# A hybrid attention layer on one core: some rounded weights and constants come by casting DMAs, probabilities are normalised in place, pairs of heads share steps, and the written order is new

## The chip, the core and the metric

The kernel runs on one core of one Trainium2 chip. The core has TensorE (PE in the profile; its weight loads are the row PEld), VectorE (DVE), ScalarE (ACT), GpSimd (POOL) and SyncE (SP), a shared on-chip memory (SBUF) of 128 partitions, and the accumulators of TensorE (PSUM), here eight banks of 128x512 float32. DMAs are issued by SP, ACT or POOL and run on 16 DMA engines.

The metric is the device time of one execution in microseconds (us), the median of several runs. The kernel before took 612.99 us (three runs: 612.47, 612.99, 614.84).

## What is computed

One decoder layer for 512 tokens of width 1024, in float32:

```python
h = rms_norm(x, pre_mix_norm)
proj = h @ w_in                                   # 1024 x 3600
att_q, att_k, att_v, gdn_qkv, gdn_z, gdn_a, gdn_b = split(proj)
o_att = moba_attention(att_q, att_k, att_v, rel_bias)   # 8 heads of 64
o_gdn = gated_deltanet(gdn_qkv, gdn_z, gdn_a, gdn_b, conv_w, A_log, dt_bias, gdn_norm_w)
mix = concat([o_att, o_gdn]) @ w_out              # 1024 x 1024
x = x + rms_norm(mix, post_mix_norm)
h = rms_norm(x, pre_mlp_norm)
m = square(relu(h @ w_up)) @ w_down               # 1024 x 4096 x 1024
return x + rms_norm(m, post_mlp_norm)
```

With 512 tokens, blocks of 256 and three past blocks allowed, the attention is plain causal softmax attention with a relative-position bias. The gated DeltaNet cuts the tokens into eight chunks of 64, needs the inverse of a unit lower triangular 64x64 matrix for each chunk and head, and then carries a 64x64 state per head through the chunks (a scan).

## The kernel before

**Three products for one.** A float32 product is made of three matmuls on rounded parts (type fp32r): hi is the rounded operand, lo is the operand minus hi, and hi·hi + hi·lo + lo·hi is summed in PSUM (`mm3`, L144). So every weight block is loaded raw by a DMA of SP, rounded by ACT (hi), and subtracted by DVE or POOL (lo): `load_split` (L121), `begun`/`ended` (L128 to 139), `split` (L112).

**Stages.** `head` (L198) does the first four projections while the norm of x is summed; PE can begin when the first x block is rounded by ACT (L240) and the first weight block by DVE (L241). `projections` (L259) does 20 more column blocks (24 matmuls of 128x512 each) and, at the item w0, the attention values of all tokens (`by_token`, 96 matmuls). After each block an evacuation runs: `conv_silu` (L359) for the DeltaNet's q, k and v, which multiplies the PSUM block in place by the norm factor, then reads it on ACT and three more times on DVE, so that the bank (tag `ps_mm`, two banks) comes free only after the third; `take_z` (L428) and `take_a` (L620) for z and for the attention's q and k.

`turned` (L513) lays scalars of one pair of heads into R, turns R by four PE transposes and makes the rows RC; `chunks` (L551) uses them for a pair of heads and ends with the chunk matrices NT and AT. The last pair's mark lets `inverse` (L735) start: 31 steps of two DVE multiplications, with its data brought through DRAM on the way in and out. `scan` (L757) reads the result, does two rounds of small matmuls, and goes through the eight chunks; after each pair of chunks `finish_o` (L885) normalises 128 tokens (its norm factor is computed by four POOL operations, L891, L171, L175, L893).

`scores` (L647) goes over four pairs of heads and three groups of query blocks (3; 2; 1 and 0): matmuls, a DVE operation that adds the bias and takes the row minimum (L675), and the exponential on ACT with the row sums (L677). After all groups DVE takes the reciprocal of the sums (L681), ACT spreads them over 512 columns (L683). `values` (L688) turns the exponentials by PE transposes (L701), ACT copies them out (L704), the spread sums are turned by four more PE transposes (L720) and copied (L722), and after the product with V DVE multiplies by them (L728) and `split` makes hi and lo.

`weights_out` (L915) loads w_out in sixteen 128x512 blocks through `load_split` (raw buffers `wo_raw`, L926), `output` (L933) multiplies (half b=0 of the columns, then b=1, for token tiles 0 and 1, then 2 and 3), `normed` (L990) adds the residual and makes the normalised input of the MLP (its two norm factors by POOL's L171 and L175), `weights_up` (L1022) and `up0` (L1039) begin the MLP. The MLP (from L1110) follows a written order of its own on all engines.

**What sets the order.** The stages above are Python generators. A list of names (`STEPS`, L20) says which generator is advanced next (`Weave.run`, L58; a name whose wait is not yet met is passed over). PE executes exactly in the order in which this emits its instructions (`manual_schedule`, L79). DVE, ACT, POOL and SP are ordered by the framework's planner from estimated times and priorities; `LEAD` (L22) raises the priority of some generators. `ORDER` (L28) is the order of the column blocks, and `LO_DVE` (L29) says which half blocks n of the projections have their lo made by DVE instead of POOL (the others by POOL). Each engine executes its own list in order: an instruction that waits holds all behind it.

## Time and profile before

| | us |
|---|---|
| median of three runs | 612.99 |
| the profiled execution's own time | 613.28 |
| its span, first to last instruction | 611.5 |
| PE busy in the span | 600.7 |
| DVE / ACT / POOL busy | 481.2 / 364.8 / 140.9 |
| granted TensorE clock, mean | 0.999 of full |
| moved by DMAs | 113.21 MB, mean 185 GB/s |

Matmuls overlap in PE's pipeline, so the duration of one (about 390 ns for 128x512) is longer than its share of PE; the distance from one start to the next is what it costs (about 227 ns). A line of the program that is a helper's stands for all who call it: L82 is every matmul, L85 every transpose, so the tile names tell them apart. In timelines each row has start, duration, engine, line, operation, what is written and read, and in brackets the idle time before and what ended it.

### The profile page before, as it was taken

The page shows a single profiled execution, that of the slowest core. Times are in us where ns is not written, and L with a number is a line of the kernel's source. Part 1 is how long each engine was busy: PE and PEld are TensorE (multiplying, and loading weights), DVE is VectorE, ACT ScalarE, POOL GpSimd, SP SyncE. Part 2 cuts the span into 40 slices and gives each one's busy share as a digit, 9 for nine tenths or more (in the row PEclk, how much of TensorE's full clock was granted, in tenths as well). Part 3 has the DMA queues.
Part 4 walks back from the last instruction along what each step waited for, and adds up shares of the span by engine and source line. Part 5 has one row for each costly group of instructions (what it writes and reads, how often), then busy time and mean ns, then how long its engine had stood idle before and what let it go on. Part 6 is the DMA issues. An engine that isn't in the chain of part 4 may idle for free.

```text
span 611.5 us, 11058 instructions
## 1 busy us (share of the span) xinstructions
PE 600.7 (98%) x4281; PEld 515.0 (84%) x4281; DVE 481.2 (79%) x692; ACT 364.8 (60%) x645; POOL 140.9 (23%) x180
## 2 busy tenths in 40 slices
PE   9999999999999999999999999999999999999995
PEld 7778788877778786888999999999998888888884
DVE  6688975999664866668799888787798888887776
ACT  7379772353677567444368565755575657565663
POOL 1557745001221111025022231122221310000000
PEclk9999999999999999999999999999999999999999
DMA  9332334227412124815879899998999999767503
GB/s 316 89 115 86 88 87 117 91 70 184 125 45 66 35 89 128 286 53 173 329 176 311 219 274 223 273 283 205 235 337 357 285 293 286 254 229 297 164 0 138
DMA packets 61156, 113.21 MB, mean 185 GB/s; under 512 B 15784, under 2 KB 35368, under 8 KB 60720
## 3 DMA queue, kind: packets, MB, share of 16 engines
q1 hardware_dynamic: 43120, 82.89, 40.0%
q0 software_dynamic: 17696, 29.36, 23.2%
q8 instruction: 33, 0.54, 0.4%
q10 hardware_dynamic: 288, 0.26, 0.1%
q14 instruction: 19, 0.16, 0.1%
HBM read 106.71 MB, written 35.15 MB: 232 GB/s over the span
## 4 chain that ended last, share of the span: by engine, by line
PE 58%; issue 9%; DMA 2%; ACT 2%; DVE 0%; POOLq 0%; SPq 0%
PE ps_mm L82 27%; PE ps_g L82 17%; PE ps_a L82 13%; DMA xy<-d_x 1%; DMA wo_raw<-in_w_out 1%; PE ps_a L85 1%; ACT wo_h L125 0%; ACT ph L704 0%; ACT L L677 0%; DVE wo_l L126 0%; DVE wdl L114 0%; ACT wdh L113 0%; PE ps_g L85 0%; POOLq L1532 0%; ACT ot L876 0%
## 5 line engine op out<-in xcount | busy, mean ns | idle before, releaser
L113 ACT CAST wdh<-wd 128x1024 fp32r<-128x1024 f32 x53 | 55.9, 1054 | 51.4 <-PE ps_mm L82 22.6
L113 ACT CAST u_h<-w 128x1024 fp32r<-128x1024 f32 x49 | 50.9, 1044 | 52.1 <-DVE w L1146 15.6
L114 DVE TENSOR_TENSOR wdl<-wd,wdh 128x1024 fp32r<-128x1024 f32 x53 | 64.9, 1224 | 21.6 <-ACT wdh L113 21.4
L114 DVE TENSOR_TENSOR u_l<-w,u_h 128x1024 fp32r<-128x1024 f32 x49 | 59.8, 1224 | 23.8 <-ACT u_h L113 23.8
L82 PE MATMUL ps_mm<-hT_h,w_hi 128*128 128x512 f32 x168 | 71.3, 424 | 1.3 <-DVE conv L365 1.0
L82 PE MATMUL ps_mm<-hT_h,w_lo 128*128 128x512 f32 x168 | 66.1, 394 | 0.0
L1179 POOL DMA_DIRECT2D d_T<-in_w_down x32 | 33.0, 1032 | 142.3 <-DMA d_T<-in_w_down 81.3
L82 PE MATMUL ps_mm<-hT_l,w_hi 128*128 128x512 f32 x168 | 65.7, 391 | 0.0
L137 ACT CAST w_hi<-w_raw 128x512 fp32r<-128x512 f32 x50 | 31.0, 620 | 46.1 <-DMA w_raw<-in_w_in 12.0
L82 PE MATMUL ps_mm<-wdh,u_h 128*128 128x512 f32 x116 | 45.3, 390 | 0.0
L82 PE MATMUL ps_mm<-wdl,u_h 128*128 128x512 f32 x116 | 45.1, 389 | 0.0
L82 PE MATMUL ps_mm<-wdh,u_l 128*128 128x512 f32 x116 | 45.1, 389 | 0.0
L82 PEld LDWEIGHTS ps_mm<-hT_h,w_hi 128*128 128x128 f32 x168 | 31.7, 189 | 12.4 <-issue 5.9
L82 PEld LDWEIGHTS ps_mm<-hT_h,w_lo 128*128 128x128 f32 x168 | 31.5, 188 | 7.5 <-DVE w_lo L138 0.4
L82 PEld LDWEIGHTS ps_mm<-hT_l,w_hi 128*128 128x128 f32 x168 | 31.8, 189 | 4.9
L138 POOL TENSOR_TENSOR w_lo<-w_raw,w_hi 128x512 fp32r<-128x512 f32 x23 | 29.7, 1291 | 20.3 <-ACT w_hi L137 17.4
L114 DVE TENSOR_TENSOR u_l<-f,u_h 128x1024 fp32r<-128x1024 f32 x28 | 34.1, 1218 | 0.0
L82 PE MATMUL ps_g<-wdh,u_h 128*128 128x512 f32 x80 | 31.1, 389 | 0.0
L82 PE MATMUL ps_g<-wdl,u_h 128*128 128x512 f32 x80 | 31.1, 389 | 0.0
L82 PE MATMUL ps_g<-wdh,u_l 128*128 128x512 f32 x80 | 31.1, 389 | 0.0
L113 ACT CAST u_h<-f 128x1024 fp32r<-128x1024 f32 x28 | 29.3, 1046 | 0.0
L138 DVE TENSOR_TENSOR w_lo<-w_raw,w_hi 128x512 fp32r<-128x512 f32 x27 | 21.4, 794 | 7.9 <-ACT w_hi L137 7.8
(486 smaller groups left out, 1830.2 us busy)
## 6 DMA issues: line engine op xcount, KB each, us to landing
d_T<-in_w_down POOLq DMA_DIRECT2D x48, 512.0 KB, 11.0
wd<-d_T SPq DMA_DIRECT2D x32, 512.0 KB, 6.2
w<-in_w_up SPq DMA_DIRECT2D x28, 512.0 KB, 7.6
wd<-in_w_down SPq DMA_DIRECT2D x24, 512.0 KB, 7.3
w_raw<-in_w_in SPq DMA_DIRECT2D x40, 256.0 KB, 2.6
wo_raw<-in_w_out SPq DMA_DIRECT2D x16, 256.0 KB, 3.5
d_T<-d_T POOLq DMA_DIRECT2D x8, 512.0 KB, 12.1
ww<-in_w_first SPq DMA_DIRECT2D x8, 256.0 KB, 5.3
```

The lines of the kernel that those rows point to most:

```text
L82: nc.tensor.matmul(o, l, r, **kw)
L85: nc.tensor.transpose(o, i, ident[:k, :k])
L113: nc.scalar.copy(hi, src)
L114: tt(lo, src, f32(hi), op=OP.subtract)
L137: nc.scalar.copy(hi, raw)
L138: (sub or tt)(lo, raw, f32(hi), op=OP.subtract)
L1179: nc.gpsimd.dma_start(d_T[t][k], block(b, second)[k], accum_op=OP.add, max_dma_last_dim=1024)
```

## The change

- **First weights.** The rounded first block (`hi0`) comes by a DMA issued by POOL that casts float32 to fp32r; DVE's rounding is gone. The raw block is still loaded for lo.
- **Constants.** The selection matrix `sel` (now nine matrices instead of five) and the mask in RC come by three such DMAs instead of plain DMAs into temporaries, POOL copies and POOL memsets.
- **conv_silu** takes a source and a place for the scaled block: for v and for q3 the place is now SBUF, so PSUM is read once.
- **Joint visits.** `turned(z)` handles two pairs of heads in one set of transposes (R has 64 used rows); a new generator `matrices(z)` makes the chunk matrices of two pairs together. `take_v` waits for the joint mark.
- **Probabilities.** After each group the reciprocal of its sums is taken and POOL multiplies each row block of exponentials by it in place; the spread sums, their four transposes per pair, their copies and the multiplication after the product are gone.
- **w_out.** The rounded blocks come by eight casting DMAs of POOL, two blocks each (512 KB); the raw blocks are still loaded and lo still subtracted by DVE; the sixteen ACT roundings are gone, and the first half has four raw buffers instead of two.
- **normed.** The product with the norm weight is formed before the norm factor is known, the factor comes from ACT's square root and DVE's reciprocal, and the residual is added in the same DVE operation that applies it.
- **up0.** Three column tiles instead of four are computed for the first half of the tokens before the last tile is normalised; the fourth is computed for all 512 tokens at the end.
- `STEPS`, `LEAD`, `ORDER` and `LO_DVE` are new; LO_DVE (19, 68) gives four more lo blocks to DVE.

```diff
-ORDER = "k0 q0 x0 y0 k1 q2 q1 k2 k3 z0 q3 x1 w0 v3 v0 v1 v2 y1 y2 x2 x3 y3 z2 z3 z1"
-LO_DVE = (23, 51)
+ORDER = "k0 q0 x0 y0 k1 q2 q1 k3 k2 z0 x1 q3 w0 v3 v1 v0 y1 v2 x2 y2 y3 x3 z1 z3 z2"
+LO_DVE = (19, 68)
...
     def head(items):
+        hi0 = wpool.tile([128, 512], FR, name="w_hi", bufs=3)
+        nc.gpsimd.dma_start(hi0, w_first[0])
...
-                (nc.scalar.copy if k else nc.vector.tensor_copy)(hi, kof(W, k))
+                if k:
+                    nc.scalar.copy(hi, kof(W, k))
...
-        for a, b in ((0, 4), (4, 5)):
-            t = tmp("cload")[:, :128 * (b - a)].rearrange("p (a b) -> p a b", b=128)
-            nc.sync.dma_start(t, c_sel[:, a:b])
-            nc.gpsimd.tensor_copy(sel[:, a:b], t)
-        mask = tmp("cload")[:, :64]
-        nc.sync.dma_start(mask, c_mask)
+        nc.gpsimd.dma_start(sel, c_sel)
         for t in RCs:
-            nc.gpsimd.memset(f32(t[32:64]), 0.0)
-            nc.gpsimd.tensor_copy(t[64:].rearrange("p (a b) -> p a b", b=64), mask[64:, None, :].to_broadcast([64, 8, 64]))
+            nc.gpsimd.dma_start(t[64:], c_mask[64:])
...
-    def conv_silu(p, ft, dst, apart=False):
-        tt(p, p, rb, op=OP.mult)
+    def conv_silu(ps, ft, p, dst, apart=False):
+        tt(p, ps, rb, op=OP.mult)
...
-            conv_silu(ps, 8 + p, v)
+            conv_silu(ps, 8 + p, v, v)
             yield
-            yield f"rkb{p}"
+            yield f"rkb{p // 2}"
...
+    def matrices(z):
+        ps = (2 * z, 2 * z + 1)
+        for p in ps:
+            yield f"E{p}"
+            yield f"q{p}"
         yield
...
+        Os = {p: within(p) for p in ps}
+        b3 = {}
+        for p in ps:
+            b3[p] = rows(p, 1)
+            for hh in range(2):
+                tt(NT[:, 2 * p + hh], Os[p][hh][:, :, 0], AT[:, 2 * p + hh], op=OP.mult)
+            if p % 2 == 0:
+                yield
...
-            nc.vector.reciprocal(sums, sums)
-            sums_of[p] = at.tile([128, 512], FT, name="R8", bufs=1)
-            nc.scalar.copy(sums_of[p].rearrange("p (q h e) -> p q h e", q=4, h=2), sums[:, :, :, None].to_broadcast([128, 4, 2, 64]))
-            mark(f"sums{p}")
+                both = slice(min(group), max(group) + 1)
+                nc.vector.reciprocal(sums[:, both], sums[:, both])
+                for q in group:
+                    for hh in range(2):
+                        l = rows_of[p, hh, q]
+                        nc.gpsimd.tensor_scalar(l, l, sums[:, q, hh:hh + 1], None, op0=OP.mult)
...
-            for q in range(4):
-                transpose(rs[:, 128 * q:128 * q + 128], sums_of[p][:, 128 * q:128 * q + 128])
...
-            mx = at.tile([128, 512], FT, name="t2")
-            tt(mx, po, sums_of[p], op=OP.mult)
-            split(mx_h[0][:, p], mx_l[0][:, p], mx)
+            split(mx_h[0][:, p], mx_l[0][:, p], po)
...
+                for k in (0, 2):
+                    nc.gpsimd.dma_start(wh[:, k:k + 2], w_out[512 * z + 128 * k:512 * z + 128 * k + 256, 512 * b:512 * b + 512].rearrange("(k p) n -> p k n", p=128))
                 for k in range(4):
...
+                    nc.sync.dma_start(raw, w_out[512 * z + 128 * k:512 * z + 128 * k + 128, 512 * b:512 * b + 512])
+                    tt(wl[:, k], raw, f32(wh[:, k]), op=OP.subtract)
...
         for b in range(2):
-            act(sq[:, 512 * b:512 * b + 512], P[b], AF.Square, accum_out=ss[:, b:b + 1])
-        tt(s1, ss[:, 0:1], ss[:, 1:2], op=OP.add)
-        r = rstd_of(s1, s1, 1024)
-        for b in range(2):
             bs = slice(512 * b, 512 * b + 512)
-            stt(sq[:, bs], P[b], r, nb[:, 0, bs], op0=OP.mult, op1=OP.mult)
-        tt(x1, x1, sq, op=OP.add)
+            act(sq[:, bs], P[b], AF.Square, scale=1 / 32, accum_out=ss[:, b:b + 1])
+            if b == 0:
+                nc.vector.tensor_scalar(ss[:, 0:1], ss[:, 0:1], EPS, None, op0=OP.add)
+            tt(sq[:, bs], P[b], nb[:, 0, bs], op=OP.mult)
+        act(s1, ss[:, 1:2], AF.Sqrt, bias=ss[:, 0:1])
+        nc.vector.reciprocal(s1, s1)
+        stt(x1, sq, s1, x1, op0=OP.mult, op1=OP.add)
...
-        r2 = rstd_of(s2, s2, 1024)
-        stt(sq, x1, r2, nb[:, 1], op0=OP.mult, op1=OP.mult)
+        act(s2, s2, AF.Sqrt, bias=epsilon)
+        nc.vector.reciprocal(s2, s2)
+        stt(sq, x1, s2, nb[:, 1], op0=OP.mult, op1=OP.mult)
...
-        for j in range(4):
-            part(j, 0, 256)
-            yield
+        for j in range(3):
+            for ks in ((range(8),) if j < 2 else (range(4), range(4, 8))):
+                part(j, 0, 256, ks)
+                yield
         yield "n3"
         for j in range(4):
-            part(j, 256, 512)
+            part(j, 256 if j < 3 else 0, 512)
```

In `turned(z)` the body is that of before, run for the pairs 2z and 2z+1 into rows 0 to 31 and 32 to 63 of R, followed by one set of four transposes and one copy, scaling and addition over 64 rows. `chunks(p)` keeps the first row product, the exponentials and their matmuls; the second row product and everything after it moved to `matrices`.

Places in the written order of PE, counted from the two step lists: between the last group of scores of pair 2 and the transposes that read it (k=1) stand, before, four projection steps (three matmuls each), one block of transposes and the first steps of the scan; now three projection steps, two blocks of transposes and the first matmuls of the scan. At the same place of pair 3 stand four projection steps and one scan step before, and seven projection steps, two scan steps and two sets of token transposes now. The last matmuls of the chunk matrices, on which `inverse` waits, come after 65 projection steps before and after 77 now.

More of the change, by code (lines that the diff above doesn't have):

```diff
@@ L23 @@
+LEAD = {'chunks': 100, 'inverse': 25, 'scan': 100, 'scores': 300, 'values': 0, 'finish_o': 300, 'take': 25, 'take_a': 25, 'scalars': 100}
 TURNS = 0, 2, 1, 3, 4, 6, 5, 7
@@ L152, in layer @@
     nc.gpsimd.memset(mhalf, -0.5)
+    epsilon = const.tile([128, 1], FT, name="eps")
+    nc.gpsimd.memset(epsilon, EPS)
     nw = const.tile([128, 1], FT, name="nw")
@@ L238, in head @@
             for k in range(8):
-                hi, lo = [wpool.tile([128, 512], FR, name=n, bufs=3) for n in ("w_hi", "w_lo")]
+                hi = wpool.tile([128, 512], FR, name="w_hi", bufs=3) if k else hi0
+                lo = wpool.tile([128, 512], FR, name="w_lo", bufs=3)
                 act(kof(hT_h, k), X[k], AF.Identity, scale=wx[:, k:k + 1])
-                (nc.scalar.copy if k else nc.vector.tensor_copy)(hi, kof(W, k))
+                if k:
+                    nc.scalar.copy(hi, kof(W, k))
                 stt(kof(hT_l, k), X[k], wx[:, k:k + 1], f32(kof(hT_h, k)), op0=OP.mult, op1=OP.subtract)
                 tt(lo, kof(W, k), f32(hi), op=OP.subtract)
+                if k == 3:
+                    nc.vector.memset(f32(sel[:, 0, :1]), 0.0)
                 if k == 4:
@@ L389, in ev @@
         def ev(ps):
-            conv_silu(ps, 4 + p, kraw[:, p])
+            conv_silu(ps, 4 + p, ps, kraw[:, p])
             yield
@@ L551, in chunks @@
     def chunks(p):
-        yield "scalars"
-        yield f"k{p}"
-        if p:
-            yield f"R{p - 1}"
-        if p > 1:
-            yield f"RC{p - 2}"
-        hp = slice(2 * p, 2 * p + 2)
-        rk = rq[0]
-        nc.gpsimd.tensor_tensor(rkb[:, :, hp], rk[:, :, hp], beta[:, :, hp], op=OP.mult)
-        nc.gpsimd.tensor_tensor(rrb[:, :, hp], rkb[:, :, hp], rk[:, :, hp], op=OP.mult)
-        mark(f"rkb{p}")
-        yield from turned(p)
-        nc.scalar.copy(RG[32 * p:32 * p + 32, p], f32(RC[p][:32, 0:512:64]))
+        yield f"RC{p // 2}"
+        yield
+        own = slice(32 * (p % 2), 32 * (p % 2) + 32)
+        nc.scalar.copy(RG[32 * p:32 * p + 32, p], f32(RC[p][own, 0:512:64]))
         b1 = rows(p, 0)
@@ L716, in values @@
             mark(f"turned{p}")
-            yield f"sums{p}"
-            rs = bank("a")
-            for q in range(4):
-                transpose(rs[:, 128 * q:128 * q + 128], sums_of[p][:, 128 * q:128 * q + 128])
-            sums_of[p] = at.tile([128, 512], FT, name="t2")
-            nc.scalar.copy(sums_of[p], rs)
+            yield
             yield
@@ L1066, in layer @@
     nc.gpsimd.memset(R, 0.0)
+    for z in range(2):
+        spawn(turned(z), LEAD["chunks"])
+        spawn(matrices(z), LEAD["chunks"])
     for p in range(4):
@@ L1072, in layer @@
     spawn(main)
-    weave.run({"inverse", "chunks3", "v0", "v1", "v2", "v3"})
+    weave.run({"inverse", "chunks1", "v0", "v1", "v2", "v3"})
     sP.close()
```

104 lines of the change are left out of this document (55 added, 49 removed).

## Prediction, made before the changed kernel was built or run

> **What bounds the kernel now.** First the page's head and its table of engines, then what PE waited for, then stretches of the span, then the chain of waits for PE's pace.
>
> ```profile
> span 611.5 us, 11058 instructions
> PE 600.7 (98%) x4281; PEld 515.0 (84%) x4281; DVE 481.2 (79%) x692; ACT 364.8 (60%) x645; POOL 140.9 (23%) x180
> ```
> ```profile
> PE ps_a L85 <- ACT L L677: 1.4, 2, 0.8
> PE ps_a L82 <- DVE rs L188: 1.1, 1, 1.1
> PE ps_mm L82 <- DVE conv L365: 1.0, 1, 1.0
> PE ps_a L82 <- DVE mins L675: 0.3, 1, 0.3
> ```
> ```profile
> 140.00:160.00 20.00, 18.67 (x91) 14.25 (x89) 17.02 (x30) 6.64 (x11) 7.36 (x7) 1.00 0.76 172
> 220.00:240.00 20.00, 18.51 (x168) 13.90 (x167) 13.31 (x28) 13.45 (x33) 5.21 (x7) 1.00 0.34 107
> 240.00:260.00 20.00, 20.00 (x90) 16.23 (x89) 13.77 (x22) 10.03 (x18) 0.00 (x0) 1.00 0.76 263
> ```
> ```profile
> 273.85 0.87 PE ps_a L85 x8
> 293.14 2.88 PE ps_g L82 x24
> 496.21 43.73 PE ps_mm L82 x192
> ```
>
> PE waits 3.8 us by these four rows (us, times, longest); a fifth, at the first weights, is shown below. The columns of the stretches are PE, PEld, DVE, ACT, POOL, then clock, DMA share and GB/s: PE is short of full only in the stretches with the named waits, and from 240 us on it never is. The chain gives its pace: 43.73/192 = 0.228 us for a matmul of 512 columns, 2.88/24 = 0.120 for 256, 0.87/8 = 0.109 for a transpose. So PE sets the end. An edit gains what it takes off PE's list or off PE's waits; relief of ACT or DVE alone gains nothing.
>
> **Less work on PE.** The sums' transposes go, 16; those of R go from 16 to 8.
>
> ```profile
> L85 PE MATMUL ps_g<-ident,R 128*128 128x128 f32 x16 | 2.5, 279 | 0.0
> L85 PE MATMUL ps_a<-ident,R 128*128 128x128 f32 x16 | 2.4, 272 | 0.0
> ```
>
> The first row is R of `turned`, the second the spread sums (both tiles are named R). 24 x 0.109 = 2.6 us. In `up0` 24 matmuls of 512 take the place of 48 of 256: 24 x (2 x 0.120 - 0.228) = 0.3. No other matmul is added or removed. Together **-2.9 us**, on PE's own list, so not hidden.
>
> **Two waits.** In the timeline of PE:
>
> ```profile
> 142.90 0.40 PE L82 MATMUL ps_mm<-hT_h,w_lo 128*128 128x512 f32 x1
> 144.28 0.47 PE L82 MATMUL ps_mm<-hT_h,w_hi 128*128 128x512 f32 x1 [0.98 <-DVE conv L365]
> 229.77 0.40 PE L82 MATMUL ps_mm<-hT_h,w_lo 128*128 128x512 f32 x1
> 230.79 0.55 PE L85 MATMUL ps_a<-ident,L 128*128 128x128 f32 x3 [0.63 <-ACT L L677]
> 232.15 0.55 PE L85 MATMUL ps_a<-ident,L 128*128 128x128 f32 x3 [0.81 <-ACT L L677]
> 232.45 0.48 PE L82 MATMUL ps_mm<-hT_h,w_hi 128*128 128x512 f32 x1
> ```
>
> From start to start the first place loses 144.28 - 142.90 - 0.23 = 1.15 us: a bank waits for the third DVE read of a v block, while `inverse` holds DVE. The new `conv_silu` copies v to SBUF in its first operation, so the bank is free two DVE operations sooner: **-1.15**.
>
> The second loses 232.45 - 229.77 - 0.23 - 6 x 0.109 = 1.8 us: transposes wait for pair 3's exponentials. There PE's list now has 7 projection steps (three matmuls, 0.68 each), 2 scan steps and 3 sets of transposes ahead, by those paces about 8 us of work, instead of 4 projection steps and a scan step, some 4.2; with the 1.8 waited the need was 6.0.
>
> ```profile
> L125 ACT CAST wo_h<-wo_raw 128x512 fp32r<-128x512 f32 x16 | 9.8, 620 | 8.3 <-DMA wo_raw<-in_w_out 8.3
> L138 POOL TENSOR_TENSOR w_lo<-w_raw,w_hi 128x512 fp32r<-128x512 f32 x23 | 29.7, 1291 | 20.3 <-ACT w_hi L137 17.4
> L334 POOL CAST picks<-cload 128x512 fp32r<-128x512 f32 x1 | 0.6, 612 | 16.9 <-DMA cload<-in_c_sel 16.9
> ```
>
> The need falls by two of w_out's roundings that stood ahead on ACT (0.62 each, 1.2) and grows by four scalings, 768 columns in all, and a short reciprocal. No row has POOL scaling 512 columns; it lies between the copy (0.61) and the subtraction (1.29), so four cost 0.9 to 1.9; I need no choice between them, since the need of 5.9 to 6.9 stays below 8: **-1.8**. Without that cover (the scalings queued behind other work of POOL) the old wait is back.
>
> **What the scaling adds.** 32 scalings, 10,240 columns, 12 to 26 us of POOL, which is idle for most of the stage; but they stand in the path of the rows, and POOL holds up DVE:
>
> ```profile
> 103.96 2.56 POOL L138 TENSOR_TENSOR w_lo<-w_raw,w_hi 128x512 fp32r<-128x512 f32 x2 [3.55 <-ACT w_hi L137]
> 103.71 0.25 DVE L748 TENSOR_TENSOR inv<-inv,pr 128x87 f32<-128x87 f32 x1
> 104.00 1.38 DVE L747 TENSOR_TENSOR pr<-inv 128x112 f32<-128x112 f32 x1
> ```
>
> A DVE product of 0.25 took 1.38 while POOL subtracted. Each scaling can stretch one DVE operation (lo of weights, the state's update) by its own length, 0.2 to 1.3. At pair 2 the new list leaves only some 4 us between the last scores and the transposes (before some 6), 3 projection steps and small work. I take **+0.9** for both, nearer the lower end, because DVE idles for over a quarter of most stretches; bounds 0 (all of it in those gaps) and 4 (2 us on PE at pair 2, which lacks that much against the old need of 6, and 2 more where the state's update is stretched). A scaling that waits for its reciprocal holds the norm factors of `finish_o` behind it on POOL, and PE's token transposes wait for those; they have half a chunk step's distance more than before, so nothing is added for them.
>
> The Trainium skill, page "SBUF — State Buffer", section "SBUF: two separate sides", says that a GpSimd operation blocks VectorE only where that one has two SBUF inputs or a two-port mode, for the whole instruction. By that rule conversions from PSUM go free and the sum is nearer its lower bound; the row at 104.00, with two SBUF inputs, agrees.
>
> **The head.** PE begins at 4.78, after the block rounded by DVE:
>
> ```profile
> 4.21 0.43 DVE L241 CAST w_hi<-ww 128x512 fp32r<-128x512 f32 x1 [3.11 <-DMA ww<-in_w_first]
> 4.78 0.77 PE L82 MATMUL ps_mm<-hT_h,w_hi 128*128 128x512 f32 x1 [0.35 <-DVE w_hi L241]
> 0.72 0.10 POOL L152 MEMSET mhalf<- 128x8 f32 x1 [0.29 <-POOLq L1528]
> L<-in_x_t SPq DMA_DIRECT2D x1, 260.0 KB, 2.8
> d_T<-g POOLq DMA_DIRECT2D x1, 1.0 KB, 4.9
> ```
>
> POOL can issue at about 0.95. No row has a casting load. By the load of its size and moment (2.8, plus 0.5 for POOL's slower issue) it lands at 4.3 and gains 0.3; by the smallest DMA of POOL (4.9) at 5.9 and costs 1.1. I take the value nearer the first, **0**, and keep -0.3 and +1.1. The constants' three DMAs take the place of POOL copies and are needed tens of us later: nothing.
>
> The Trainium skill, page "DMA: Bandwidth & Descriptors", section "Anatomy of one DMA", fits a GpSimd DMA as 2.0 us plus bytes over 436,000. By it 256 KB take an estimated 2.6 us and the sum would fall by 0.3; the row of 4.9 for 1 KB disagrees, beside other traffic.
>
> **w_out by POOL.** Eight DMAs of 512 KB come on top of the raw loads.
>
> ```profile
> 213.00:227.00 14.00, 14.00 (x172) 11.47 (x169) 9.38 (x20) 8.89 (x21) 2.79 (x4) 1.00 0.25 82
> 227.00:241.00 14.00, 12.51 (x88) 8.60 (x86) 9.36 (x22) 11.63 (x27) 2.79 (x4) 1.00 0.35 109
> 241.00:255.00 14.00, 14.00 (x64) 11.59 (x63) 10.36 (x17) 6.24 (x11) 0.00 (x0) 1.00 0.95 329
> q0 software_dynamic: 17696, 29.36, 23.2%
> ```
>
> POOL's queue moved 29.36 MB in 0.232 x 611.5 = 142 us of all engines, 207 GB/s, so 4.2 MB take 20 us of them. From 213 to 241 about 70% are free, 19.6 us: it just fits. I take **0**: that spare time hides it. A cast that waits for its buffer holds POOL's scalings and norm factors behind it, and with them PE's transposes. Gone, the spare time costs a wait of PE at the second half of w_out; bounds 0 and 10 (second rival).
>
> **Costed at nothing.** `normed`: the last tile's chain ends just before PE needs it.
>
> ```profile
> 293.80 1.28 DVE L1007 SCALAR_TENSOR_TENSOR xs<-xs,s,nb 128x1024 f32<-128x1024 f32 x1 [0.98 <-POOL s L175]
> 295.86 1.04 PE L85 MATMUL ps_a<-ident,xs 128*128 128x128 f32 x8
> ```
>
> It is done at 295.08 and PE comes at 295.86. POOL's two visits (the wait of 0.98 shows one) become shorter steps on ACT and DVE, and an addition over 1024 columns is folded into the next operation, so the chain is 2 to 3 us shorter, while PE's list gives it 1.4 us less (half an `up0` block of 2.88): the cover grows from 0.8 to over 1. `up0`'s work hides it; gone, its lateness goes to PE one for one. ACT's 9.8 us of roundings and the copies of sums lay beside PE's work. Four lo blocks moved to DVE are four subtractions more there, under projections; joint visits remove two sets of small operations. The stores of NT stay on SP's queue and leave later, with the chunk matrices (third rival). SP loses three small loads, which nobody waits for.
>
> Sum: -2.9 - 1.15 - 1.8 + 0.9 = -4.95, from 613.28 (the profiled execution: span 611.5 and 1.8 around it) to 608.3. The median lies 0.3 lower, so **608.0 us**.
>
> **Rivals.**
>
> *More gain, 604.5.* The new order also ends the small waits (mins 0.3) and the gaps around the scan's first rounds, the scaling costs nothing, the head gains 0.3: -0.9 - 0.3 - 0.3 and up to 2 more. For it: such gaps exist in 140 to 180; against: PE's list there is as dense as before.
>
> *Slower, 618.* w_out arrives late. Its second half needs buffers that the projections' operands hold until they end. From then 2.1 MB by POOL (10 us) and 2.1 MB raw share the engines with the next loads, in a stretch that already has a DMA share of 0.95. If the casts are issued only then, the last blocks come some 10 us after PE wants them: 608 + 10. It decides when the first block of half 1 lands later than PE's first use of it, which is 14 x 0.68 = 9.6 us after the first product with w_out begins. Against it: half 0 can be fetched early.
>
> *No change, 612.* The inverse is late. Before:
>
> ```profile
> L764 SPq DMA_DIRECT2D uap<-d_t x4: 430/486/487, 150.8 to 152.4; - x4
> DMA to landing us min/median/max: 3.9/4.4/5.0
> 166.98 1.31 PE L82 MATMUL ps_g<-uap,NT 32*32 32x32 f32 x128
> ```
>
> Its data land at 156.8 and PE uses them at 167.0, a reserve of 10.2. It now starts 12 projection steps (8 us) later and PE comes about a microsecond earlier: reserve 1. Should DVE lose another 5 us to blocked products, PE waits 4 and the gain is gone. Against: it no longer meets the three subtractions of POOL at 104 to 110.
>
> **Chances.** Forecast 0.47 (606 to 610), more gain 0.17 (602 to 606), no change 0.23 (610 to 616), slower 0.13. Faster by over 0.5% (below 609.9; 3 us are about what a measurement of this kernel tells from none) 0.64, within 0.23, slower 0.13. The range 603.0 to 615.0 leaves out the rest of the first rival and the last.
>
> **What would show it.** In the new profile: no wait of PE for conv; no transposes of sums; the wait at pair 3's transposes gone, and one for a POOL scaling at pair 2, below 1 us; PE's first product at 4.5 to 5.9; full stretches from 240 us on. A wait of PE on w_out's blocks or for uap, or a first product after 6, makes the prediction wrong.

## The result: 619 us, and the profile after

The changed kernel takes **618.92 us** (median of 7 runs) against **612.99** before. It is slower by 0.94%: the ratio is 1.0094, with a 95% interval of 1.0074 to 1.0114. The profiled execution took 617.84. One of the seven runs took 842.45 at a granted TensorE clock of 0.658; the ratios here and below leave such slow runs out, among them the profiled one of e14_relief (0.665), which is why that kernel has no span in the table.

The head of the page, and what PE waited for (us in all, times, longest):

```profile
span 615.9 us, 10995 instructions
PE 598.7 (97%) x4233; PEld 511.9 (83%) x4233; DVE 478.3 (78%) x706; ACT 353.1 (57%) x625; POOL 168.9 (27%) x195
```
```profile
PE ps_mm L82 <- DMA w_hi<-in_w_first: 2.6, 1, 2.6
PE ps_a L85 <- POOL L L694: 1.3, 3, 0.7
PE ps_g L82 <- ACT mg_h L112: 1.3, 1, 1.3
PE ps_a L82 <- DVE rs L187: 1.1, 1, 1.1
PE ps_g L82 <- DVE S L878: 1.0, 1, 1.0
PE ps_mm L82 <- POOL w_lo L135: 0.9, 2, 0.7
PE ps_mm L82 <- DVE conv L365: 0.8, 1, 0.8
PE ps_g L82 <- DVE mg_l L113: 0.6, 1, 0.6
PE ps_g L85 <- DVE ot L900: 0.5, 1, 0.5
PE ps_g L82 <- DVE LWQ L568: 0.3, 1, 0.3
```

PE's busy time fell by 2.0 us (600.7 to 598.7, 48 instructions fewer). Its idle time, span less busy, rose by 6.4 (611.5 - 600.7 = 10.8 to 615.9 - 598.7 = 17.2). The two make the 4.4 us by which the span grew. The waits named come to 10.4 us, against 4.1 in the five rows of before: what idle time was added is waits, and the list says for whom.

The same stretches as before (PE, PEld, DVE, ACT, POOL, clock, DMA share, GB/s):

```profile
140.00:160.00 20.00, 19.89 (x94) 15.67 (x93) 19.77 (x51) 8.86 (x17) 0.38 (x1) 1.00 0.24 79
220.00:240.00 20.00, 18.97 (x176) 15.64 (x176) 12.72 (x30) 10.40 (x29) 13.13 (x17) 1.00 0.56 174
240.00:260.00 20.00, 17.55 (x78) 12.68 (x74) 12.23 (x19) 4.53 (x10) 3.36 (x4) 1.00 1.00 340
```

The two stretches that the change was to fill are fuller: 19.89 of 20 for 18.67, and 18.97 for 18.51. The third was full before and now lacks 2.45 us, with the DMA engines at 1.00. The wait for conv in the list is not the old one at 144 us: it stands at 48.70.

**At the start**, in the timeline:

```profile
1.29 0.73 POOL L199 DMA_DIRECT2D w_hi<-in_w_first  x1 [0.43 <-issue]
2.48 1.10 POOL L338 DMA_DIRECT2D RC<-in_c_mask  x2
7.07 0.77 PE L82 MATMUL ps_mm<-hT_h,w_hi 128*128 128x512 f32 x1 [2.63 <-DMA w_hi<-in_w_first]
7.23 0.72 ACT L242 ACTIVATE hT_h<-xx,L 128x512 fp32r<-128x512 f32 x1 [3.02 <-DMA xx<-in_x_t]
8.91 0.63 PE L82 MATMUL ps_mm<-hT_l,w_hi 128*128 128x512 f32 x1
```

The casting DMA is issued at 1.29, and PE waits 2.63 us for it. The first product comes at 7.07 instead of 4.78. The products behind the gap are long ones: 0.63 where 0.39 is usual. Two of the constants' casting DMAs (the mask, 128 KB each) are issued here too, at 2.48, among the first loads; the second x block is there at 7.23, where it was there at 5.28 before.

**The scalings**, all shapes together and then the longest alone (busy, mean ns | idle before):

```profile
L694 POOL TENSOR_SCALAR L<-L,sums 128x512 f32<-128x512 f32 (+3 forms) x32 | 38.3, 1210 | 54.0 <-DVE inv L754 44.9 <-DVE sums L690 9.0
```
```profile
L694 POOL TENSOR_SCALAR L<-L,sums 128x512 f32<-128x512 f32 x8 | 13.7, 1725 | 45.9 <-DVE inv L754 44.9 <-DVE sums L690 1.0
```

They take 38.3 us of POOL. One of 512 columns takes 1.73, more than the subtraction of 1.29 that was to be the upper bound. The waits for POOL's rows, which the prediction expected as one below 1 us, are three of 0.3 to 0.7.

**At w_out's second half**, the timeline of three engines:

```profile
226.53 0.69 DVE L900 TENSOR_TENSOR ot<-ot,oss 128x512 f32<-128x512 f32 x1 [3.56 <-POOL oss L899]
233.68 4.26 POOL L694 TENSOR_SCALAR L<-L,sums 128x256 f32<-128x256 f32 x4 [5.64 <-DVE sums L690]
237.89 1.47 POOL L931 DMA_DIRECT2D wo_h<-in_w_out  x2
241.94 1.52 POOL L931 DMA_DIRECT2D wo_h<-in_w_out  x2
246.22 1.29 DVE L937 TENSOR_TENSOR wo_l<-wo_raw,wo_h 128x512 fp32r<-128x512 f32 x2 [2.97 <-DMA wo_h<-in_w_out]
248.03 0.74 DVE L909 SCALAR_TENSOR_TENSOR om<-ps_g,nw,zs 128x512 f32<-128x512 f32 x1
249.48 0.50 PE L82 MATMUL ps_g<-wo_h,mg_h 128*128 128x512 f32 x1 [1.32 <-ACT mg_h L112]
```

The first row is a norm factor of `finish_o`: DVE waits 3.56 us for it, since POOL began it at 223.98, behind two scalings from 220.76 on. Two subtractions of w_out and the state S stand behind it on DVE, and PE waits 1.03 for S at 229.38. From the second row on: POOL issues the casting DMAs only behind the last scalings. DVE's next subtraction waits 2.97 us for one of them. Behind it in DVE's order stands `om` of `finish_o`, then mg_h and mg_l, and PE waits for those. The late transfer isn't what PE asks for; what queues behind it is.

### The profile page after: what moved, and what is told of

Its sections match the earlier page's. It is cut to its first block, busy times and chain, and to the rows that moved or that the text cites. A ratio compares the mean times of both kernels' runs of the same rounds, so it can differ in the third digit from the quotient of the medians.

```text
span 615.9 us, 10995 instructions
## 1 busy us (share of the span) xinstructions
PE 598.7 (97%) x4233; PEld 511.9 (83%) x4233; DVE 478.3 (78%) x706; ACT 353.1 (57%) x625; POOL 168.9 (27%) x195
## 4 chain that ended last, share of the span: by engine, by line
PE 53%; issue 11%; POOL 4%; DMA 3%; DVE 1%; ACT 0%; POOLq 0%; SPq 0%
PE ps_mm L82 24%; PE ps_g L82 16%; PE ps_a L82 12%; POOL L L694 2%; DMA wo_h<-in_w_out 2%; PE ps_a L85 1%; DMA xy<-d_x 1%; POOL kdec L813 1%; POOL wo_h L931 0%; POOL oss L174 0%; DVE wo_l L937 0%; DVE wdl L113 0%; POOL kB L812 0%; ACT wdh L112 0%; DVE zs L436 0%
## 5 line engine op out<-in xcount | busy, mean ns | idle before, releaser
L694 POOL TENSOR_SCALAR L<-L,sums 128x512 f32<-128x512 f32 (+3 forms) x32 | 38.3, 1210 | 54.0 <-DVE inv L754 44.9
L135 POOL TENSOR_TENSOR w_lo<-w_raw,w_hi 128x512 fp32r<-128x512 f32 x19 | 24.7, 1300 | 25.8 <-ACT w_hi L134 23.2
```

The costliest lines, as they stand in the source:

```text
L135: (sub or tt)(lo, raw, f32(hi), op=OP.subtract)
L694: nc.gpsimd.tensor_scalar(l, l, sums[:, q, hh:hh + 1], None, op0=OP.mult)
```

## Experiments

Theories: **A**, the casting DMA of the first block costs the head some 3 us. **B**, the scalings on POOL cost more than 0.9. **C**, the casting DMAs of w_out hold DVE, and with it `finish_o`. Rival **D**: the new written order and the joint visits cost by themselves. PE's order is written out, but the planner orders ACT, DVE, POOL and SP by its own estimate of times, so that an edit can move instructions far from it; several runs show this. The spans and idle times are those of one profiled execution each; verdicts go by the ratios.

| Run | Median, us | Ratio to before (95%) | Span, us | PE idle, us |
|---|---|---|---|---|
| changed kernel | 618.92 | 1.0094 (1.0074 to 1.0114) | 615.9 | 17.2 |
| e1_head | 616.84 | 1.0056 (1.0037 to 1.0076) | 612.9 | 15.3 |
| e2_sums | 623.81 | 1.0192 (1.0156 to 1.0229) | 622.3 | 21.0 |
| e3_wout | 623.48 | 1.0167 (1.0143 to 1.0191) | 622.3 | 20.2 |
| e4_all3 | 621.93 | 1.0150 (1.0125 to 1.0176) | 618.1 | 18.1 |
| e5_dve | 616.06 | 1.0057 (1.0038 to 1.0076) | 616.2 | 18.2 |
| e6_act | 623.90 | 1.0186 (1.0160 to 1.0211) | 619.8 | 22.5 |
| e7_bpool | 639.37 | 1.0433 (1.0414 to 1.0452) | 636.8 | 28.7 |
| e8_bdve_v | 619.04 | 1.0105 (1.0085 to 1.0126) | 619.9 | 17.2 |
| e9_noscale | 617.35 | 1.0086 (1.0052 to 1.0120) | 616.2 | 15.9 |
| e10_split | 617.72 | 1.0084 (1.0056 to 1.0112) | 615.8 | 18.5 |
| e11_b_v | 613.81 | 1.0018 (1.0002 to 1.0033) | 612.7 | 11.4 |
| e12_wopool | 615.48 | 1.0050 (1.0030 to 1.0070) | 613.4 | 15.2 |
| e13_noscale_sp | 613.71 | 1.0011 (0.9999 to 1.0023) | 610.2 | 14.1 |
| e14_relief | 614.77 | 1.0029 (1.0018 to 1.0041) | none | none |
| e15_relief_act | 614.75 | 1.0031 (1.0020 to 1.0043) | 612.8 | 14.7 |
| e16_b_wout | 619.99 | 1.0124 (1.0102 to 1.0146) | 617.8 | 14.5 |
| e17_diag | 622.81 | 1.0168 (1.0154 to 1.0182) | 620.7 | 14.0 |
| e18_b_diag | 626.15 | 1.0227 (1.0212 to 1.0241) | 624.4 | 15.2 |

**The head alone undone.**

```diff
-        nc.gpsimd.dma_start(hi0, w_first[0])
-                if k:
-                    nc.scalar.copy(hi, kof(W, k))
+                (nc.scalar.copy if k else nc.vector.tensor_copy)(hi, kof(W, k))
```

> The changed kernel with one part undone: DVE rounds the first block of w_first again, and its casting DMA is gone. Theory A (the casting DMA holds the first product from 4.8 to 7.1 us, and the longer idle time makes twice as many slow matmuls behind it): first product at 4.8, excess of PE in the first 10 us back from 5.9 to about 2.9, time about 3.0 us less, near 616. Rival (the x blocks land later for another reason, so the wait only moves to the second block): at most 0.5 us less, near 618.5.

In its timeline the first product is back at 4.91, and is as short as the rest:

```profile
4.91 0.47 PE L82 MATMUL ps_mm<-hT_h,w_hi 128*128 128x512 f32 x1 [0.48 <-DVE w_hi L242]
```

The span is 3.0 us shorter. By the ratios the gain is 0.0038 x 612.7 = 2.3 us, and the two intervals just touch. Theory A holds. The start is not quite as before, though: in the first 20 us PE is busy for 17.95, against 18.57 before and 16.29 in the changed kernel. The mask's two casting DMAs are still issued there (1.32), the second x block is there at 7.13, and PE waits 0.50 for the weights rounded behind it. In all profiled kernels that have these DMAs the block is there at 6.4 to 8.2 us, in those that don't at 5.3 to 6.7; no run takes them out alone. Most of what follows in the new order starts from this kernel.

**The other parts undone.** e2_sums brings the late sums back, e3_wout load_split for w_out, e4_all3 all three; the diffs are those of the change, reversed.

> The changed kernel with one part undone: the probabilities are not scaled in place; their sums are spread and transposed, and the output is multiplied, as before. PE has 16 transposes more, +1.7 us. Theory B (the 32 scalings on POOL, 38.3 us, delay the kernel by queueing: POOL comes late to w_out's casting DMAs and to the norm factors): the wait of 0.9 at 186 us, that at 228 us and most of the 2.9 us between 242 and 251 us go, some 4 to 5 us, so the time falls by 2 to 3 us, near 616. Rival (w_out's casts are late by themselves, because their buffers come free late): these waits stay, the 16 transposes come on top, near 620.5.

> The changed kernel with one part undone: w_out is rounded by ACT from the raw blocks again, and its eight casting DMAs are gone; the raw blocks keep the buffers of the changed kernel. Theory C (the casting DMAs land late, and the subtractions that wait for them stand on DVE ahead of finish_o's work): the three waits of PE between 242 and 251 us go, about 2.9 us, near 616. Rival (finish_o is late because POOL's scalings hold its norm factors, and the roundings on ACT make the last exponentials later): the waits stay in other places, within 1 us of 619.

> All three parts undone at once (first block by DVE, late sums, w_out by ACT). What is left of the change: the new written order, the joint visits, the constants by casting DMAs, the v blocks through SBUF, normed. PE's list is 1.2 us shorter than before the change. Theories A, B and C together: near 612, no slower than before. Rival D (the new order and the joint visits themselves cost the time): 615 or more, with waits of PE between 40 and 190 us that the kernel before had not.

All three are slower than the changed kernel, which theories A to C had not expected; of e4_all3 D had (615 or more, with new waits between 40 and 190 us: 2.7 at 174 and 1.8 at 181). Undoing a part takes the old work into a written order that was made for the new. In e2_sums PE lost most at 175 us, and the row behind it has nothing to do with sums:

```profile
175.58 0.62 ACT L134 CAST w_hi<-w_raw 128x512 fp32r<-128x512 f32 x1 [4.27 <-DMA w_raw<-in_w_in]
```

A load of w_in had slipped on SP behind loads of the scan. ACT waited 4.27 for it, with the copies of the transposed rows behind it. In e4_all3 the same load is late (ACT waits 3.95 at 171 us), just ahead of the waits that D had expected; in e3_wout it is not, and PE lost most to mg_h (3.1). So these three runs price no part, and D stays open. Two other ways were needed: the parts alone in the old order, and leaving work out with the orders held.

**The scalings on another engine**, in e1_head:

```diff
-                        nc.gpsimd.tensor_scalar(l, l, sums[:, q, hh:hh + 1], None, op0=OP.mult)
+                        nc.vector.tensor_scalar(l, l, sums[:, q, hh:hh + 1], None, op0=OP.mult)
```

e6_act has `act(l, l, AF.Copy, scale=...)` in its place, e10_split POOL for the first head and DVE for the second.

> As e1_head (first block rounded by DVE), and the 32 scalings run on DVE instead of POOL. Theory B (the scalings cost because POOL does them slowly, 1.21 us each: the rows come late, POOL's subtractions of weights wait behind them, and w_out's casting DMAs are issued behind them): against e1_head the waits on POOL at 63 to 70 us (1.2) and at 168 to 185 us (some 2) go, and most of the 2.1 between 245 and 248 us: near 611 to 612. Rival (the scalings are too much for any engine in the path of the rows; on DVE, the fullest beside PE, they delay the state's update and the subtractions): no gain over e1_head, 614 to 617, with waits for DVE instead.

> As e5_dve, with the 32 scalings on ACT. Theory B: the same waits on POOL go, and ACT, idle for over 40% of the span, has room: near 612. Rival (ACT stands in the path of the rows already with the exponentials and the copies of the transposed blocks, so 32 operations more of some 0.6 us make the copies late): waits of PE for ACT in 165 to 190 us and 235 to 245 us, 614 or more.

> As e1_head, with each pair of scalings shared: the first head's on POOL, the second's on DVE. If the length of POOL's pair of scalings (2 x 1.21 us in the mean) is what PE waits for, the rows come about half of that sooner and POOL is free sooner for w_out's casting DMAs: 2 to 3 us below e1_head, 612 to 613. Rival (POOL and DVE hold one another up, or DVE is late for its own work as with all of them on DVE): 614.5 or more.

By their times the rivals were right in all three. The operation is far shorter elsewhere: this row of e5_dve, then that of e6_act, against 1,725 ns on POOL.

```profile
L692 DVE TENSOR_SCALAR L<-L,sums 128x512 f32<-128x512 f32 x8 | 4.3, 579 | 0.0
```
```profile
L692 ACT ACTIVATE L<-L,sums 128x512 f32<-128x512 f32 x8 | 5.3, 714 | 0.4 <-DVE sums L688 0.3
```

The waits for POOL's rows went. Others came, for copies, `ot` and `pt`. But the mechanism of the rivals, a busier engine that is late, isn't shown: in all three the load of w_in slipped again (ACT waits 2.3 to 2.8 us for it at 172 to 175 us), and the longest wait, 5.1 us of PE for `ot` in e10_split, comes from a casting DMA of w_out, behind which `om` and `ot` stand on DVE:

```profile
240.37 0.69 DVE L935 TENSOR_TENSOR wo_l<-wo_raw,wo_h 128x512 fp32r<-128x512 f32 x1 [4.67 <-DMA wo_h<-in_w_out]
```

**Parts alone in the old order.** e7_bpool puts the scalings on POOL into the kernel before:

```diff
+                both = slice(min(group), max(group) + 1)
+                nc.vector.reciprocal(sums[:, both], sums[:, both])
+                for q in group:
+                    for hh in range(2):
+                        l = rows_of[p, hh, q]
+                        nc.gpsimd.tensor_scalar(l, l, sums[:, q, hh:hh + 1], None, op0=OP.mult)
                 yield
...
-            tt(mx, po, sums_of[p], op=OP.mult)
-            split(mx_h[0][:, p], mx_l[0][:, p], mx)
+            split(mx_h[0][:, p], mx_l[0][:, p], po)
```

> The kernel before with one part of the change alone: the probabilities are scaled in place by POOL, the sums' spread, their 16 transposes and the multiplication are gone; the old written order. PE's list is 1.7 us shorter. Prediction's price of the scaling (+0.9): about 612.2, or 610.4 if the wait at pair 3 goes too. Theory B (POOL's 1.21 us per scaling cost several us): a wait of PE for POOL at each pair's transposes, those of pair 3 longer than the 1.8 us of before: 614 to 617.

It costs 26.5 us (0.0433 x 612.7). Not all of that is waiting: PE is busy for 608.1 us, 7.4 more than before with 16 transposes fewer, since its products are long behind waits of this length (last section). PE's waits, and the timeline of POOL and PE at pair 0:

```profile
PE ps_g L85 <- ACT R L516: 8.6, 2, 4.8
PE ps_a L85 <- POOL L L683: 7.9, 6, 3.0
```
```profile
58.90 2.98 POOL L683 TENSOR_SCALAR L<-L,sums 128x256 f32<-128x256 f32 x4
65.75 0.20 POOL L560 TENSOR_TENSOR rkb<-rk,beta 128x8 f32<-128x8 f32 x1
69.62 1.12 PE L85 MATMUL ps_g<-ident,R 128*128 128x128 f32 x4 [3.79 <-ACT R L516]
```

About half of these two rows isn't in the path of the rows of probabilities at all. The keys' norm factors stand behind the scalings on POOL, `turned` needs them, and PE waits twice for R. In the changed kernel, where these visits are joint and later, PE has no wait for R.

e8_bdve_v scales by DVE in the old order and has the v blocks through SBUF, e11_b_v the v blocks alone:

```diff
-    def conv_silu(p, ft, dst, apart=False):
-        tt(p, p, rb, op=OP.mult)
+    def conv_silu(ps, ft, p, dst, apart=False):
+        tt(p, ps, rb, op=OP.mult)
...
-            conv_silu(ps, 8 + p, v)
+            conv_silu(ps, 8 + p, v, v)
```

> The kernel before with two parts of the change alone and one of them altered: the probabilities are scaled in place by DVE, and conv_silu copies the v blocks to SBUF in its first operation; the old written order. PE's list is 1.7 us shorter, the wait of 1.15 us at 143 us goes. If both parts are worth what the prediction gave them and DVE does the scaling at little cost: 610. Rival (rows come later by the scaling, so the wait at pair 3's transposes grows, and DVE delays the rest): 612 or more.

> The kernel before with one part of the change alone: conv_silu copies the v blocks to SBUF in its first operation; the old written order. By the prediction the wait for conv at 143 us goes, 1.15 us: 611.4. Rival (the wait moves to the next bank or to the transposes of v, for which PE then comes earlier): within 0.5 of 612.6.

In e11_b_v the wait for conv at 143 us is gone, and this one, no shorter, is new:

```profile
PE ps_g L85 <- DVE vt L370: 1.3, 1, 1.3
```

Freeing the bank brought PE sooner to the transposes of v, which wait for the same chain on DVE. That is the rival's mechanism; its time, within 0.5 of 612.6, was missed too. e8_bdve_v has the same wait, and a longer one for its rows:

```profile
PE ps_a L85 <- DVE L L683: 3.7, 2, 3.0
```

e16_b_wout has only w_out's casting DMAs, with the two raw buffers of before where the changed kernel has four:

```diff
+                for k in (0, 2):
+                    nc.gpsimd.dma_start(wh[:, k:k + 2], w_out[512 * z + 128 * k:512 * z + 128 * k + 256, 512 * b:512 * b + 512].rearrange("(k p) n -> p k n", p=128))
                 for k in range(4):
...
-                    load_split(wh[:, k], wl[:, k], w_out[512 * z + 128 * k:512 * z + 128 * k + 128, 512 * b:512 * b + 512],
-                               raw=wpool.tile([128, 512], FT, name="wo_raw", tag=tag, bufs=bufs))
+                    raw = wpool.tile([128, 512], FT, name="wo_raw", tag=tag, bufs=bufs)
+                    nc.sync.dma_start(raw, w_out[512 * z + 128 * k:512 * z + 128 * k + 128, 512 * b:512 * b + 512])
+                    tt(wl[:, k], raw, f32(wh[:, k]), op=OP.subtract)
```

> The kernel before with one part of the change alone: w_out's rounded blocks come by eight casting DMAs from POOL's queue; the old written order, no scaling on POOL. The prediction's price is nothing, and ACT's relief would shorten the wait at pair 3: 611 to 612.6. Theory C (the casting DMAs land late by themselves, behind their buffers and the other loads, and hold DVE's subtractions with finish_o's work behind them): waits of PE of 2 to 3 us after 240 us, 614.5 or more.

It costs 7.6 us (0.0124 x 612.7). Its DMA issues (KB each, median us to landing), then DVE, ACT and PE in the timeline:

```profile
wo_h<-in_w_out POOLq DMA_DIRECT2D x8, 512.0 KB, 7.5
wo_raw<-in_w_out SPq DMA_DIRECT2D x16, 256.0 KB, 5.2
```
```profile
231.20 0.69 DVE L930 TENSOR_TENSOR wo_l<-wo_raw,wo_h 128x512 fp32r<-128x512 f32 x1 [4.82 <-DMA wo_raw<-in_w_out]
232.88 0.51 ACT L677 ACTIVATE L<-L,mins 128x256 f32<-128x256 f32 x1 [5.82 <-DVE mins L675]
233.53 0.69 PE L85 MATMUL ps_a<-ident,L 128*128 128x128 f32 x2 [3.23 <-ACT L L677]
```

The raw loads, 3.5 us to landing in the kernel before, take 5.2 beside the casting ones. DVE waits 4.82 for one, with pair 3's scores behind it; PE waits 3.23 for the exponentials that follow from them. So w_out's casting DMAs cost time without any scaling on POOL, and by holding DVE, as theory C says. But its path is only the smaller part here: the largest wait goes by a raw load and pair 3's scores, and `finish_o` (`om` and mg_l, after 240 us) makes 1.9 us. And of the 6.3 us by which the span is longer, 2.6 are PE's busy time: the granted clock is 0.83 from 220 to 240 us.

**The scalings left out.** e9_noscale is e1_head without the four lines of the loop that scales, so its output lacks the division by the sums. e13_noscale_sp also gives the loads of w_in from number 30 on a higher rank with the planner, which keeps SP's order as it is in e1_head:

```diff
-        nc.sync.dma_start(v(raw), src)
+        with tc.high_priority(lead) if lead else ExitStack(): nc.sync.dma_start(v(raw), src)
...
-        begin = lambda n: begun(w_in[items[n // 2][0] // 128, :, 4 * (n % 2):4 * (n % 2) + 4], (4, 128))
+        begin = lambda n: begun(w_in[items[n // 2][0] // 128, :, 4 * (n % 2):4 * (n % 2) + 4], (4, 128), lead=300 * (30 <= n < 99))
```

> As e1_head, with the 32 scalings left out: the output lacks the division by the softmax sums (the reciprocals are still made). So it gives the whole price of the scalings in the new order. Theory B (they are most of what is left over the kernel before): the waits of PE at 63 to 70, 168 to 185 and 225 us go, and with POOL free w_out's casting DMAs are issued up to 4 us earlier, so part of the 2.1 us between 245 and 248 goes: near 610, 4 to 5 below e1_head. Rival D (the new order costs by itself): 613 or more.

> As e9_noscale (head undone, the 32 scalings left out, so the output lacks the division by the sums), with SP's order of loads held as in e1_head: in e9_noscale two loads of w_in had slipped behind the scan's loads and E's, and PE lost 3.4 us at 171 us to that alone. Theory B (the scalings are the price): 4 us below e9_noscale and 3 below e1_head, 611 to 613. Rival D (without them the new order is no better than the old one; other waits stay): 614.5 or more.

e9_noscale missed for the reason of e2_sums: ACT waits 4.56 us for the same load at 171.77.

With SP's order held the ratio falls to 1.0011. So in the new order the scalings cost 0.0045 x 612.7 = 2.8 us (from the two intervals, 1.4 to 4.2): theory B. Gone are e1_head's waits for POOL's rows (1.4) and for w_lo, which POOL subtracts behind the scalings (0.9). But this kernel, without scalings, without the casting DMA at the head and with 2.9 us less on PE, is no faster than the kernel before. Its waits say why, and the timeline of DVE and ACT:

```profile
PE ps_a L82 <- ACT ph L715: 1.3, 1, 1.3
PE ps_mm L82 <- DVE mg_l L113: 1.0, 1, 1.0
PE ps_g L85 <- DVE om L907: 0.9, 1, 0.9
```
```profile
229.86 1.90 DVE L935 TENSOR_TENSOR wo_l<-wo_raw,wo_h 128x512 fp32r<-128x512 f32 x3 [2.68 <-DMA wo_raw<-in_w_out]
234.48 0.63 ACT L433 ACTIVATE t<-zs 128x512 f32<-128x512 f32 x1 [2.35 <-DVE zs L431]
235.01 1.05 ACT L715 COPY ph<-ps_a 128x512 f32<-128x512 f32 x2
```

These three, 3.2 us, stand between 235 and 241 us. There DVE works off the subtractions of w_out that a late load had held up; `zs` stands behind them, ACT waits for it, and the copies of the rows stand behind that.

**Relief.** e12_wopool gives w_out's last eight subtractions to POOL. e14_relief gives it four of them, and takes two of w_in's off it; e15_relief_act adds ACT for one of the two longest scalings of each pair.

```diff
-LO_DVE = (19, 68)
+LO_DVE = (17, 68)
...
-                    tt(wl[:, k], raw, f32(wh[:, k]), op=OP.subtract)
+                    (nc.gpsimd.tensor_tensor if b and z else tt)(wl[:, k], raw, f32(wh[:, k]), op=OP.subtract)
```

> As e1_head, with the eight subtractions of w_out's second half of columns on POOL instead of DVE. Theory C (DVE stands idle for the casting DMAs from 240.7 to 243.4 us with finish_o's work behind it in its order): DVE is free for om and mg_l, the waits of PE for mg_h and mg_l between 245 and 248 us (2.1) go; POOL's 1.3 us per block just keeps pace with PE: 612.5 to 613. Rival (POOL's blocks come late, or DVE is blocked while POOL subtracts): waits of PE for w_lo's blocks from 250 us on, 615 or more.

> As e1_head, with two things taken out of POOL's and DVE's way: two subtractions of w_in that stood behind pair 0's scalings go from POOL to DVE, and the four subtractions of w_out's second columns that finish_o's work stood behind go from DVE to POOL. If the waits of PE at 63 to 68 us (1.2) and at 245 to 248 us (2.1) are due to those two queues, both go: 3 us below e1_head, 612 to 613.5. Rival (they move to the next block): no gain, 615.5 or more.

> As e14_relief, with one of each pair's two longest scalings (512 columns, 1.7 us on POOL) on ACT, and SP's order held. If the rows of the first group are late by POOL's second scaling, the waits of 0.5 and 0.9 at 168 and 184 us go too: 1 us below e14_relief, 611.5 to 612.5. Rival (ACT's copies and exponentials come later by as much): as e14_relief or more.

e12_wopool loses the waits for mg_h and mg_l, and has three for POOL's blocks of wo_l instead, 1.4 us in all: the rival was right.

e14_relief gains 0.0027 x 612.7 = 1.7 us over e1_head, about half of what was expected; ACT's share adds nothing that can be measured. These are the best kernels with the change in them, and still 0.3% slower than the kernel before (e13_noscale_sp, which is at 1.0011, leaves the division out).

**The division in the transposes.** e17_diag and e18_b_diag write the reciprocal sums on a diagonal and multiply by it where the rows were transposed (R is narrower in both, to make room in SBUF):

```diff
-                        nc.gpsimd.tensor_scalar(l, l, sums[:, q, hh:hh + 1], None, op0=OP.mult)
+                        nc.vector.tensor_scalar(diag[:, 2 * q + hh], ident, sums[:, q, hh:hh + 1], None, op0=OP.mult)
...
-                            transpose(tp[:, o:o + 128], rows_of[p, hh, q][:, 128 * k:128 * k + 128])
+                            mm(tp[:, o:o + 128], rows_of[p, hh, q][:, 128 * k:128 * k + 128], diag_of[p, hh, q], start=True, stop=True)
```

> As e13_noscale_sp, with the division put back at another place: DVE writes the reciprocal sums on the diagonal of a 128x128 block for each row block, and the block is transposed by a product with that diagonal in place of the identity, so the rows wait for 128 columns instead of up to 512 and POOL does nothing for it. If the price of the scalings is their length in the rows' path and POOL's queue, this costs little over e13_noscale_sp (613.7): 613 to 614.5. Rival (32 operations more of some 0.28 us on DVE, as its scaling of 128 columns took in e5_dve, delay its other work as in e5_dve): 615.5 or more.

> The kernel before, the old written order, with the sums' spread, their 16 transposes and the multiplication replaced by the same products with diagonals. PE's list is 1.7 us shorter, ACT loses eight copies of 512 columns. If the old order bears it, 611 (the version that would beat both kernels). Rival (as in e8_bdve_v, the rows of pair 3 come later by DVE's work and PE waits for them): 614 or more.

Both missed. The rivals had the sign, but not the reason: PE's idle time in e17_diag is no longer than in e13_noscale_sp (14.0 against 14.1), and its busy time is 10.6 us longer. The group of e13_noscale_sp, then that of e17_diag:

```profile
L85 PE MATMUL ps_a<-ident,L 128*128 128x128 f32 x80 | 11.4, 274 | 0.0
```
```profile
L82 PE MATMUL ps_a<-diag,L 128*128 128x128 f32 x160 | 20.9, 277 | 2.3 <-ACT ph L718 1.6 <-DVE ma_l L113 0.7
```

A product in f32 is two instructions on PE where a transpose is one: 80 more of 0.109 us, 8.7 us by that pace. Without them e17_diag's span would be an estimated 612.0. No kernel here beats the one before.

## Why the prediction was wrong

Forecast 608.0, range 603.0 to 615.0; the time is 618.92. The steps that failed are the three that the sum took at nothing or little: w_out's DMAs (0), the scaling (+0.9) and the head (0). The first cost some 3 us by the rows of e13_noscale_sp, the others 2.8 and 2.3 by runs. By the prediction's steps:

- **Less work on PE, -2.9: right.** 48 instructions fewer; in e1_head PE's busy time is 3.1 us below that of before. In the changed kernel it is 2.0; the long products at the start are part of the difference.
- **The wait on conv, -1.15: not shown to be the edit's.** In the changed kernel the wait at 144 us is gone and its stretch gains 1.22 us, but the order is new too. Alone the edit gains nothing (e11_b_v): the wait goes to the transposes of v. The step didn't ask what is late next.
- **The wait at pair 3, -1.8: right as far as it went.** It is gone. A wait of 1.0 for the state S (L878), behind a norm factor and w_out's subtractions, stands in the same stretch, which gains 0.46 us.
- **The scaling, +0.9 within 0 to 4: mis-sized.** The term was bounded by a copy and a subtraction, 12 to 26 us of POOL; it is 38.3, since the scaling with one input is slower on POOL than the subtraction with two. It measured 2.8 in the new order, three times the term but within its bounds, and 26.5 in the old, slow products included; the new order is spared most of that. The step named the norm factors of `finish_o` behind the scalings and added nothing for them; the row at 226.53 shows one that holds DVE, and with it PE. Those of the keys, behind which PE waits for R in e7_bpool, it left out.

  The Trainium skill, page "GPSIMD Engine Reference", section "4.1 Engine selection", holds one-input operations on GpSimd to be roughly at line rate. Here the scaling of 512 columns took 1,725 ns on POOL, 579 on DVE and 714 on ACT, so for this operation the measurement decides otherwise.
- **POOL blocking DVE, part of the same term: small.** DVE's busy time is 479.3 us in e1_head and 477.5 in e13_noscale_sp, so the scalings stretch its work by about 1.8 us in all. The Trainium skill, page "SBUF — State Buffer", section "SBUF: two separate sides", has a GpSimd operation block VectorE only where that one has two SBUF inputs or a two-port mode. The trace agrees: the four kinds of operation that grew most (the two subtractions of weights, `vt` and `zs`, 1.4 us together) all have two SBUF inputs.
- **The head, 0 within -0.3 to +1.1: mis-sized.** It measured 2.3 by time and 3.0 by span. Between a load of the same size (2.8) and a small DMA of POOL (4.9) the step took the first; the casting load took 5.6. A first product after 6 us was named as what would make the prediction wrong, and it came at 7.07. The constants' three DMAs, taken at nothing as needed much later, are in part issued beside the first loads; by the rows above PE waits 0.2 to 1.6 us for the second block in most kernels that have them without the first one.
- **w_out by POOL, 0 within 0 to 10: the step failed.** It added up free DMA time and found that the transfers just fit. Each may still come later: raw loads took 5.2 instead of 3.5 us in the old order; in the changed kernel they keep 3.5, but the casting ones take 7.7 in the median and up to 13.4. What counts is which instruction of DVE waits for them and what stands behind it. In the old order that costs 7.6 us. In the new one it shows as the waits for mg_h, mg_l and ot (2.4 us). The rival "w_out arrives late", given 0.13, had the time (618) and the late issue, but not the mechanism: PE waits for `finish_o`, hardly for w_out. That its number fits is luck: of the 5.8 us lost, 2.3 are the head's and 2.8 the scalings'.
- **normed and ACT's relief at nothing: right.** No wait of PE stands at 290 to 300 us. ACT has 11.7 us less to do, and nothing came of it. The joint visits were not tried alone.
- **The inverse late, 0.23: did not happen.** PE has no wait for uap.

By the ratios, then, the 5.8 us (0.0094 x 612.7) are 2.3 for the head, 2.8 for the scalings and 0.7 of e13_noscale_sp, in which 2.9 us of saved work are set against some 3.6 of waits. By the rows of e13_noscale_sp these are 6.3 us of new waits less the 2.7 of before that are gone (pair 3, conv at 144 us, mins): 3.2 are w_out's, 1.1 are the second block's at the start, and 2.0 (`vn`, `conv`, LWQ) may be the new order's own. That is argued from the rows and not separated by a run. Rival D is thus not refuted; by these rows the new order gives about as much as it takes. So the two savings of waits did come, and what failed is the step that let nothing else come late in their place.

## What to carry to other kernels

Where one engine is nearly full, ask of each operation that you give to another engine what stands behind it in that engine's order, and who waits for that; idle time and free bandwidth of the helper say little. Price an operation on an engine by a row of that operation on that engine, and where there is none, measure it before moving 32 of them. A part that is undone in an order made for it prices nothing: try it alone in the old order, or leave its work out with the other queues held.

## What the runs showed of the hardware

**PE slows down after short gaps, and not always.** In e11_b_v two waits of 0.6 and 0.8 us within 2 us are followed by a run of long products:

```profile
231.99 0.90 PE L85 MATMUL ps_a<-ident,L 128*128 128x128 f32 x3 [0.81 <-ACT L L677]
233.12 0.63 PE L82 MATMUL ps_mm<-hT_l,w_hi 128*128 128x512 f32 x1
```

From start to start these products take 0.42 us instead of 0.23, until 235.25, and the granted clock from 220 to 240 us is 0.91. The kernel before has the same two waits (0.63 and 0.81), no slow products behind them and a clock of 1.00. In e7_bpool, behind waits of 3.8 and 4.8 us, the granted clock of a stretch shows it (the third number from the end):

```profile
40.00:72.00 32.00, 23.43 (x114) 18.20 (x113) 18.35 (x44) 21.53 (x58) 24.61 (x30) 0.85 0.28 83
```

The Trainium skill, page "TensorE: Matmul & The Clock Gate", section "What's actually happening", has the clock halved after an idle window of about 3.4 us that runs freely. The factor of nearly two agrees; that it takes an idle time of that length doesn't, since here 0.6 and 0.8 us were enough once.

**A load's size does not set when it lands.** The first of these rows is the casting DMA, the second the plain load that SP issues first, the third the seven behind it (changed kernel, DMA issues):

```profile
w_hi<-in_w_first POOLq DMA_DIRECT2D x1, 256.0 KB, 5.6
L<-in_x_t SPq DMA_DIRECT2D x1, 260.0 KB, 2.7
xx<-in_x_t SPq DMA_DIRECT2D x7, 256.0 KB, 6.8
```

Equal bytes landed after 2.7 to 6.8 us. POOL's DMA is issued among the later ones and lands like them; whether the casting itself adds to that was not tried.
